# Forty lo subtractions and eight block additions go from VectorE to GpSimd

## Chip, cores and metric

The kernel runs on one core of a Trainium2 chip. The metric is the device time of one launch in microseconds (us). A core has five engines, each with its own in-order instruction queue: TensorE (PE, matmuls), VectorE (DVE), ScalarE (ACT), GpSimd (POOL) and SyncE (SP, which here only issues DMA transfers). ACT and POOL issue transfers too. An instruction that waits holds up everything behind it in its queue.

## The reference, cut to what matters

One layer of a streaming encoder with D = T = 1024 and float32 throughout:

```python
h = rms_norm(x, norm_mix_g) * (1.0 + sc1) + sh1
b_s, c_s, v_s, v_c, gl_c, gate_br = split(h @ w_in)
y_a = (b_s * causal_dwconv(c_s * v_s, conv_short_w)) @ w_short_out
u = causal_dwconv(v_c * sigmoid(gl_c), conv_conf_w) + conv_conf_b
y_b = silu(layer_norm(u, conf_ln_g, conf_ln_b)) @ w_conf_out
g_a, g_b = split(sigmoid(gate_br))
x = x + g1 * ((g_a * y_a + g_b * y_b) @ w_o)
...
x = x + g2 * ((silu(a) * bgate) @ w_ffn_out)
```

The change is in the two branch projections, `y_a` and `y_b`, and in the mix, the product with `w_o`.

## The kernel before

**Products in parts.** A float32 product is made of three matmuls in the fast format fp32r: operand and weight are each split into a hi part (the rounded value) and a lo part (what the rounding left), and hi x hi, hi x lo and lo x hi are added up in PSUM (`mm3`, L380, L381, L383). For a weight block, `split_w` makes the parts: ACT casts the loaded block (tile `raw`) to `wh` (L226), and `lo_engine` subtracts it from the block to make `wl` (L227). There are three buffers for `wh`, three for `wl` and five for `raw` in a ring; a new part waits until the product that used its buffer is through, and a new load waits until the last reader of its `raw` is.

**Products of seven.** The combined projection, the first branch projection, and the feed-forward block do a 2 x 2 block product with seven products of halves instead of eight (Strassen in Winograd's form). The names "1" to "7" in `PRODUCTS = "1265734"` are these. Some need sums of weight blocks, so a unit of the plan is a load, perhaps block additions, a hi cast and a lo subtraction. The first branch projection has two halves `d`, each with its seven: `ya_order` runs "1", "1", "2", "2" of both, then "6", "5", "7", "3", "4" of the first half and of the second. `apart_units` (L298) makes its units: two additions before "6", one each before "7" and "3" (all in `add`, L304).

**The plan.** `plan` is a list of weight units in the order of use. `next_w` hands out the next and keeps `AHEAD = 2` more made ahead. The kernel's program order is then rearranged by a scheduler that decides each engine's queue; semaphores keep the dependencies.

**The stages around the change** (times of the profile before). To 565.6 us: the combined projection, whose weights' lo parts are made by POOL, while DVE does the width-31 convolution (`conv`, L902, accumulators in PSUM). 565.6 to 645.6: the first branch projection, 14 products of 24 matmuls. In it DVE splits the operands (`q_split`, L850) and does their sums (`q_sum`), prepares the layer norm (`ln_square`: L945, L951; `ln_rstd`) and evacuates products (`ya_evac`: L737, L740, L744), with gate values `ga` that POOL's queue loads (L1016). The first half's products "2", "5" and "3" share one pair of banks (called y and z), products "6", "7", "4" another (x). 645.6 to 732.6: the second branch projection in two halves of 512 columns (`row_blocks`): eight weight units for the first half, of which three are kept, and five more for the second. Before each product `act_b` scales an operand (L982, with `rl0` for the first half and `rl1` for the second), applies silu on ACT and splits it (L413). `load_b` and `modulation_of` (L361) use DVE and the `raw` buffers for unrelated modulation sums. The gate loads `gb` (L1072, POOL's queue) take six shared small buffers (`gs`), two of which hold `rl0` and `rl1` until their last use. 732.6 to 820.5: the mix, 16 products, with loads of `xr` (L1087) and stores of the result (L1095) on POOL's queue. Then the feed-forward block, which the change leaves alone.

Of the kernel before, what the change touches and what calls it, by code (L numbers as in the profile page):

```python
# [44 lines left out]
KC = D // P  # L45
# [29 lines left out]
KEPT = 3  # L75
SECOND = [*range(KC - KEPT, KC), *range(KC - KEPT)]
# [51 lines left out]
def block_kernel(ctx: ExitStack, tc: tile.TileContext, x0, xT, c, vecs, ada, w_first, w_plain, w_duals,  # L128
                 w_short, w_conf, w_o, w_fi, w_fo, w_last, outT):
    nc = tc.nc  # L130
# [74 lines left out]
    def raw_tile(n=1024):  # L205

        raws.append(raws.pop(0))
        return raws[-1].tile([P, 1024], F32, tag="raw", name="raw")[:, :n]

    def load(src, n=1024):  # L210
        raw = raw_tile(n)
        load.ins = nc.sync.dma_start(raw, src).ins
        return raw
# [6 lines left out]
    def split_w(raw, n, after=(), lo_engine=nc.vector):  # L220
        wh = whp.tile([P, 1024], F32R, tag="wh", name="wh")[:, :n]
        wl = wlp.tile([P, 1024], F32R, tag="wl", name="wl")[:, :n]
        with ExitStack() as order:
            for ins in after:
                order.enter_context(tc.issue_after(ins))
            hi = nc.scalar.copy(wh, raw)  # L226
            lo = lo_engine.tensor_tensor(wl, raw, f32(wh), ALU.subtract)  # L227
        split_w.hi, split_w.lo = hi.ins, lo.ins
        if n == T and lo_engine is nc.gpsimd:
            pool_los.append((hi.ins, lo.ins))  # L230
        return wh, wl
# [66 lines left out]
    def apart_units(mats, eng):  # L298


        a = {}

        def add(out, x, y):
            eng.tensor_tensor(out, x, y, ALU.add)  # L304
            return out

        def get(b):
            return load(mats[("11", "12", "21", "22").index(b)])

        def unit(m):  # L310
            if m in "12":
                raw = get("1" + m)
            elif m == "6":
                for b in ("21", "22", "11"):
                    a[b] = get(b)
                a["s1"] = add(a["22"], a["21"], a["22"])
                raw = a["s2"] = add(raw_tile(), a["11"], a["s1"])
            elif m == "7":
                raw = add(a["21"], a["21"], a["11"])
            elif m == "3":  # L320
                raw = get("12")
                add(raw, raw, a["s2"])
            else:
                raw = a["s1"] if m == "5" else get("22")
            return split_w(raw, 1024, (), eng)

        return {m: (lambda m=m: unit(m)) for m in PRODUCTS}


    plan = [None] * KC  # L330
# [2 lines left out]
        units = dual_units([w_duals[d, m] for m in range(4)], 1024, eng=nc.gpsimd)  # L333
        plan += [units[m] for m in PRODUCTS]
    ya_order = [(d, m) for m in "12" for d in range(2)] + [(d, m) for d in range(2) for m in PRODUCTS[2:]]
    ya_units = [apart_units([w_short[d, m] for m in range(4)], nc.vector) for d in range(2)]
    plan += [ya_units[d][m] for d, m in ya_order]
    plan += [(w[k], 1024) for w in (w_conf, w_o) for ks in (range(KC), SECOND[KEPT:]) for k in ks]
    ready = []

    def next_w(ahead=AHEAD):
# [1195 lines left out]
```

## Time and profile before

| | before |
|---|---|
| device time, median of 3 | 1471.18 us (1470.85 to 1472.19) |
| span of the profiled execution, first to last instruction | 1469.8 us |
| mean granted TensorE clock | 0.998 |
| GpSimd busy | 515.7 us |
| VectorE busy | 1178.7 us |

The span is the time from the first instruction of the profiled execution to its last; its own device time is not listed apart, and the median of the runs lies 1.4 us above the span. Groups are read as: line, engine, operation, tiles written and read, shapes and count; then busy time and mean ns of one; then the idle time of the engine before them and what ended it. Rows of the timeline give the start, the length, the engine and the instructions (several of one kind in a row are merged). Rows of a window table give from and to, the length, then busy time and count of PE, weight loads (PEld), DVE, ACT and POOL, the granted clock, the DMA share and GB/s. A row of waits says who waited for what: us in total, times, longest.

### The profile page before, as it was taken

The page shows a single profiled execution, that of the slowest core. Times are in us where ns is not written, and L with a number is a line of the kernel's source. Part 1 is how long each engine was busy: PE and PEld are TensorE (multiplying, and loading weights), DVE is VectorE, ACT ScalarE, POOL GpSimd, SP SyncE. Part 2 cuts the span into 40 slices and gives each one's busy share as a digit, 9 for nine tenths or more (in the row PEclk, how much of TensorE's full clock was granted, in tenths as well). Part 3 has the DMA queues.
Part 4 walks back from the last instruction along what each step waited for, and adds up shares of the span by engine and source line. Part 5 has one row for each costly group of instructions (what it writes and reads, how often), then busy time and mean ns, then how long its engine had stood idle before and what let it go on. Part 6 is the DMA issues. An engine that isn't in the chain of part 4 may idle for free.

```text
span 1469.8 us, 17768 instructions
## 1 busy us (share of the span) xinstructions
PE 1459.0 (99%) x6447; PEld 1197.9 (81%) x6447; DVE 1178.7 (80%) x1625; ACT 615.0 (42%) x896; POOL 515.7 (35%) x464
## 2 busy tenths in 40 slices
PE   9999999999999999999999999999999999999997
PEld 5888888888888888888888888888888888888887
DVE  8999888887998969999688798777777765676755
ACT  5753433333433346455235474444444443222325
POOL 0046677767777771111022002101111115435005
PEclk9999999999999999999999999999999999999999
DMA  9412213222222258376596336654555449999403
GB/s 373 165 59 72 101 58 129 72 86 101 101 67 78 93 205 303 115 239 215 194 315 221 106 106 233 221 170 163 168 185 173 158 154 373 341 287 280 139 15 115
DMA packets 83913, 247.97 MB, mean 169 GB/s; under 512 B 9665, under 2 KB 11713, under 8 KB 83826
## 3 DMA queue, kind: packets, MB, share of 16 engines
q1 hardware_dynamic: 43072, 138.63, 28.3%
q0 software_dynamic: 37008, 95.63, 19.8%
q10 hardware_dynamic: 3746, 12.59, 2.3%
q8 instruction: 50, 0.82, 0.2%
q14 instruction: 37, 0.30, 0.1%
HBM read 184.41 MB, written 62.39 MB: 168 GB/s over the span
## 4 chain that ended last, share of the span: by engine, by line
PE 97%; DVE 1%; POOL 0%; issue 0%; ACT 0%; POOLq 0%; DVEq 0%
PE bank L383 12%; PE bank L380 12%; PE bank L381 12%; PE x L381 8%; PE x L383 8%; PE x L380 7%; PE z L380 4%; PE z L383 4%; PE z L381 4%; PE y L381 3%; PE y L380 3%; PE y L383 3%; PE mix L383 2%; PE mix L380 2%; PE yb L383 2%; PE yb L380 2%
## 5 line engine op out<-in xcount | busy, mean ns | idle before, releaser
L226 ACT CAST wh<-raw 128x1024 fp32r<-128x1024 f32 (+2 forms) x253 | 255.2, 1010 | 454.9 <-PE bank L381 129.9
L227 POOL TENSOR_TENSOR wl<-raw,wh 128x1024 fp32r<-128x1024 f32 x84 | 204.8, 2446 | 82.1 <-ACT wh L226 82.1
L227 DVE TENSOR_TENSOR wl<-raw,wh 128x1024 fp32r<-128x1024 f32 (+2 forms) x169 | 193.6, 1146 | 37.4 <-ACT wh L226 36.1
L902 DVE SCALAR_TENSOR_TENSOR c<-diff,vec,c 128x512 f32<-128x512 f32 x232 | 171.0, 752 | 4.4
L1250 POOL DMA_DIRECT2D hid<-stage x71 | 37.9, 534 | 345.4 <-DVE stage L421 341.1
L380 PE MATMUL bank<-th,wh 128*128 128x512 f32 x288 | 112.0, 389 | 0.0
L381 PE MATMUL bank<-tl,wh 128*128 128x512 f32 x288 | 112.0, 389 | 0.0
L383 PE MATMUL bank<-th,wl 128*128 128x512 f32 x288 | 112.0, 389 | 0.0
L902 DVE SCALAR_TENSOR_TENSOR c<-u,wsum,c 128x512 f32<-128x512 f32 x112 | 84.3, 753 | 2.6
L420 ACT CAST stage<-g 128x512 fp32r<-128x512 f32 x62 | 38.4, 622 | 84.0 <-DVE g L1239 41.9
L246 POOL TENSOR_TENSOR raw<-raw 128x1024 f32<-128x1024 f32 x12 | 29.2, 2433 | 125.1 <-DVE wl L227 87.7
L421 DVE TENSOR_TENSOR stage<-g,stage 128x512 fp32r<-128x512 f32 x62 | 42.4, 689 | 26.9 <-ACT stage L420 26.8
L381 PEld LDWEIGHTS bank<-tl,wh 128*128 128x128 f32 x288 | 54.1, 188 | 11.3
L383 PEld LDWEIGHTS bank<-th,wl 128*128 128x128 f32 x288 | 54.1, 188 | 11.2
L380 PEld LDWEIGHTS bank<-th,wh 128*128 128x128 f32 x288 | 54.1, 188 | 11.2
L1276 POOL DMA_DIRECT2D th<-hid x71 | 38.1, 537 | 52.8 <-PE x L383 29.3
L380 PE MATMUL x<-th,wh 128*128 128x512 f32 x144 | 56.1, 390 | 0.1
L383 PE MATMUL x<-th,wl 128*128 128x512 f32 x144 | 56.0, 389 | 0.0
L381 PE MATMUL x<-tl,wh 128*128 128x512 f32 x144 | 56.0, 389 | 0.0
L246 DVE TENSOR_TENSOR raw<-raw 128x1024 f32<-128x1024 f32 (+1 forms) x17 | 19.2, 1129 | 42.2 <-DMA raw<-in_w_fi 31.6
L380 PE MATMUL yb<-zsh,wh 128*128 128x512 f32 x128 | 49.8, 389 | 0.0
L381 PE MATMUL yb<-zsl,wh 128*128 128x512 f32 x128 | 49.8, 389 | 0.0
(811 smaller groups left out, 4243.9 us busy)
## 6 DMA issues: line engine op xcount, KB each, us to landing
hid<-stage POOLq DMA_DIRECT2D x71, 512.0 KB, 4.6
raw<-in_w_fi SPq DMA_DIRECT2D x54, 512.0 KB, 4.4
raw<-in_w_duals SPq DMA_DIRECT2D x48, 512.0 KB, 3.5
th<-hid POOLq DMA_DIRECT2D x71, 256.0 KB, 5.7
tl<-hid POOLq DMA_DIRECT2D x71, 256.0 KB, 5.7
ada<-in_ada SPq DMA_DIRECT2D x24, 512.0 KB, 5.5
raw<-in_ada SPq DMA_DIRECT2D x24, 512.0 KB, 4.5
raw<-in_w_fo SPq DMA_DIRECT2D x24, 384.0 KB, 5.8
```

Of the source, the lines that this page charges most:

```text
L226: hi = nc.scalar.copy(wh, raw)
L227: lo = lo_engine.tensor_tensor(wl, raw, f32(wh), ALU.subtract)
L246: eng.tensor_tensor(a["s1"], a["21"], a["22"], ALU.add)
L380: nc.tensor.matmul(ps, wh, xh, start=first, stop=False, skip_group_check=again)
L381: nc.tensor.matmul(ps, wh, xl, start=False, stop=False, skip_group_check=again)
L383: mm3.ins = nc.tensor.matmul(ps, wl, xh, start=False, stop=last, skip_group_check=again).ins
L420: t_split.act = nc.scalar.copy(hi, src).ins
L421: t_split.ins = nc.vector.tensor_tensor(lo, src, f32(hi), ALU.subtract).ins
L902: tap.ins = nc.vector.scalar_tensor_tensor(out=out, in0=src[:, s : s + H], scalar=wt, in1=acc, op0=ALU.mult, op1=ALU.add).ins
L1250: nc.gpsimd.dma_start(hid_dram[key], s)
L1276: nc.gpsimd.dma_start(t, hid_dram[key][:, s])
```

## The change

```diff
     ya_order = [(d, m) for m in "12" for d in range(2)] + [(d, m) for d in range(2) for m in PRODUCTS[2:]]
-    ya_units = [apart_units([w_short[d, m] for m in range(4)], nc.vector) for d in range(2)]
+    ya_units = [apart_units([w_short[d, m] for m in range(4)], nc.gpsimd) for d in range(2)]
     plan += [ya_units[d][m] for d, m in ya_order]
-    plan += [(w[k], 1024) for w in (w_conf, w_o) for ks in (range(KC), SECOND[KEPT:]) for k in ks]
+    plan += [(w[k], 1024, (), nc.gpsimd) for w in (w_conf, w_o) for ks in (range(KC), SECOND[KEPT:]) for k in ks]
```

The engine that `apart_units` hands to its additions and to `split_w` is GpSimd instead of VectorE, and the units of `w_conf` and `w_o` name GpSimd as the engine of their lo part. The hi casts stay on ACT, the loads on SP. That is 14 + 13 + 13 = 40 subtractions and 2 x 4 = 8 additions, each on 128 x 1024 elements. The scheduler places them in GpSimd's queue among the transfers that it issues; the order of VectorE's other work changes a little with it.

## The prediction

> **What bounds the kernel now.** I read the busy times and the chain of waits first, then who TensorE (PE) waits for.
>
> ```profile
> PE 1459.0 (99%) x6447; PEld 1197.9 (81%) x6447; DVE 1178.7 (80%) x1625; ACT 615.0 (42%) x896; POOL 515.7 (35%) x464
> PE 97%; DVE 1%; POOL 0%; issue 0%; ACT 0%; POOLq 0%; DVEq 0%
> ```
> ```profile
> PE clock L573 <- DVE ones_r L591: 1.6, 1, 1.6
> PE x L381 <- DVE t4l L421: 0.5, 1, 0.5
> PE clock L573 <- DVE newton L450: 0.2, 1, 0.2
> ```
>
> PE is on the chain for 97% of the span, and the three rows are all that it waits for: 2.3 us, none of it in the stages that the change touches. The busy times of these stages, as windows (PE, weight loads, VectorE = DVE, ScalarE = ACT, GpSimd = POOL): two windows of the first branch projection, two halves of the second, two of the mix.
>
> ```profile
> 565.50:594.50 29.00, 29.00 (x126) 23.31 (x125) 28.82 (x41) 21.49 (x38) 2.18 (x4) 1.00 0.72 248
> 594.50:645.50 51.00, 51.00 (x221) 41.12 (x220) 48.70 (x68) 26.19 (x36) 7.53 (x14) 1.00 0.52 170
> 645.50:689.00 43.50, 43.50 (x193) 36.02 (x193) 42.83 (x66) 24.93 (x35) 3.65 (x7) 1.00 0.74 240
> 689.00:732.50 43.50, 43.50 (x194) 36.02 (x193) 31.52 (x47) 13.78 (x19) 3.88 (x8) 1.00 0.59 194
> 732.50:776.00 43.50, 43.50 (x194) 36.02 (x193) 35.12 (x58) 13.69 (x19) 8.67 (x16) 1.00 0.84 288
> 776.00:820.50 44.50, 44.50 (x196) 36.49 (x195) 32.82 (x43) 24.12 (x34) 8.13 (x15) 1.00 0.65 209
> ```
>
> PE is full and at full clock everywhere, so there is nothing to win. DVE is full too until 689, with little slack towards PE, while POOL is nearly free. The question is whether POOL can take the work without making DVE late.
>
> **What it costs DVE when POOL computes.** POOL did such subtractions before, in the combined projection. In the first fence are POOL's and DVE's operations of all times, in the second those between 543.5 and 557.4, where POOL's last ones of that stage meet DVE work with two inputs in SBUF; the third has the same DVE forms some microseconds later, with POOL idle.
>
> ```profile
> L227 POOL TENSOR_TENSOR wl<-raw,wh 128x1024 fp32r<-128x1024 f32 x84 | 204.8, 2446 | 82.1 <-ACT wh L226 82.1
> L902 DVE SCALAR_TENSOR_TENSOR c<-diff,vec,c 128x512 f32<-128x512 f32 x232 | 171.0, 752 | 4.4
> ```
> ```profile
> L850 DVE TENSOR_TENSOR q<-q,q1h 128x512 fp32r<-128x512 f32 x4 | 6.9, 1786 | 0.0
> L425 DVE SCALAR_TENSOR_TENSOR q<-q,q 128x512 f32<-128x512 f32 x4 | 6.9, 1775 | 0.0
> L227 POOL TENSOR_TENSOR wl<-raw,wh 128x1024 fp32r<-128x1024 f32 x3 | 8.2, 2753 | 7.3 <-ACT wh L226 7.3
> L923 POOL TENSOR_TENSOR tot<-tot,u 128x512 f32<-128x512 f32 x2 | 3.4, 1742 | 0.0
> ```
> ```profile
> 558.61 2.48 DVE L425 SCALAR_TENSOR_TENSOR q<-q,q 128x512 f32<-128x512 f32 x4
> 587.14 2.49 DVE L850 TENSOR_TENSOR q<-q,q3h 128x512 fp32r<-128x512 f32 x4
> ```
>
> Four such operations take 2.5 us alone (0.6 each) and 6.9 us beside POOL. The eight lost 13.8 - 4.8 = 9.0 us to three long and two short POOL operations; shared out by these lengths (2753 to 1742) that is 2.1 us for each long one. POOL loses only 2753 - 2446 = 0.3 us. The two engines alternate: one DVE operation gets through for each POOL operation. The convolution's taps (L902, accumulator in PSUM, 752 ns through all that POOL did) are not touched, so operations with an operand in PSUM are free of it. In the stages of the change most DVE work is of the endangered kind: the q splits (L850), L945, L951, L982, L413, L1061.
>
> [...]
>
> **What moves.** 40 subtractions (14 for the first projection, 13 each for the second and the mix) and 8 block additions. Rows of DVE between 557.4 and 591.8:
>
> ```profile
> L227 DVE TENSOR_TENSOR wl<-raw,wh 128x1024 fp32r<-128x1024 f32 x6 | 7.3, 1215 | 0.0
> L304 DVE TENSOR_TENSOR raw<-raw 128x1024 f32<-128x1024 f32 x4 | 4.9, 1218 | 0.2 <-DMA raw<-in_w_short 0.2
> ```
>
> DVE is freed of 1.14 us each (1.22 less the 0.08 in which neighbours overlap): 55 us. POOL gets 48 x 2.45 = 118 us, and each costs DVE 2.1 us wherever DVE has no gap: a net loss of 1.0 us each. Removed ACT work, PE work, loads: none. In the changed order the additions and subtractions also share POOL's queue with the gate loads (L1016, L1072), the x loads (L1087) and the x1 stores (L1095), which wait for buffers and results.
>
> **First place: the second use of the y banks.** Product "5" of the first half (starts at 594.53) writes the bank that L740 must have read.
>
> ```profile
> 557.41 1.28 DVE L737 TENSOR_TENSOR sig<-bank,sig 128x512 f32<-128x512 f32 x2
> 571.10 1.21 DVE L304 TENSOR_TENSOR raw<-raw 128x1024 f32<-128x1024 f32 x1
> 591.88 1.28 DVE L740 TENSOR_TENSOR ma<-bank,ga 128x512 f32<-128x512 f32 x2
> 607.32 1.28 DVE L737 TENSOR_TENSOR z<-bank,vz 128x512 f32<-128x512 f32 x2
> ```
> ```profile
> 594.53 0.39 PE L380 MATMUL bank<-q5h,wh 128*128 128x512 f32 x1
> 610.91 0.39 PE L380 MATMUL bank<-q4h,wh 128*128 128x512 f32 x1
> ```
> ```profile
> 578.42 28.16 SPq L212 DMA_DIRECT2D raw<-in_w_short  x6
> ```
>
> Slack today: 594.5 - 592.5 (end of L740's first) = 2 us. In the new order 40 DVE operations stand between 557.4 and L740: 24.1 us. Six subtractions and four additions of POOL come with them: two before 571, when the first addition can run (today's L304), then eight in a row, 8 x 2.8 = 22 us, until 593.5. Three more follow before DVE is through: the seventh subtraction, the next half's first addition, the eighth subtraction; the SP row says that raw buffers are short, so they come with gaps. L740 then runs at 557.4 + 24.1 + 13 x 2.1 = 608.8, and PE waits 608.8 - 594.5 = **14.3 us**. Low end: ten POOL operations, four DVE ones with PSUM hidden under them: 557.4 + 24.1 + 21 - 2.4 = 600.1, a wait of 5.6. High end: fourteen, 16.4.
>
> **Second place: product "4" of the first half**, due 16.4 us after product "5", writes the x bank that L737 (607.32 now) must have read. 25 DVE operations stand between: 15.1 us, with four or five POOL operations, 9.5 us, less 1.2 hidden: 23.4 - 16.4 = **7.0 us** more. Low 1 (one POOL operation), high 10. After it POOL waits for gate loads whose buffers DVE frees, and DVE catches up: I cost the way to the second projection at nothing. Its cover is the slack of zsl, 645.55 - 640.34 = 5.2 us; without it each POOL operation there costs 2.1 us less 1.1.
>
> ```profile
> 639.65 0.69 DVE L413 TENSOR_TENSOR zsl<-cv,zsh 128x512 fp32r<-128x512 f32 x1 [0.18 <-ACT zsh L412]
> ```
> ```profile
> 645.55 0.39 PE L380 MATMUL yb<-zsh,wh 128*128 128x512 f32 x1
> 679.33 0.39 PE L383 MATMUL yb<-zsh,wl 128*128 128x512 f32 x1
> ```
>
> **Third place: the last subtraction of the second projection's first half** now stands in POOL's queue behind the sixth gate load, which waits until DVE has used rl1 for the last time (L982).
>
> ```profile
> 645.97 1.31 DVE L744 SCALAR_TENSOR_TENSOR ma<-bank,ga 128x512 f32<-128x512 f32 x2 [0.91 <-DMA ga<-gate_a]
> 676.90 3.10 DVE L982 TENSOR_TENSOR cv<-cv,rl1r 128x512 f32<-128x512 f32 x5
> 680.30 0.54 POOL L1072 DMA_DIRECT2D gb<-gate_b  x1 [16.73 <-DVE cv L982]
> ```
> ```profile
> L227 DVE TENSOR_TENSOR wl<-raw,wh 128x1024 fp32r<-128x1024 f32 x6 | 7.3, 1221 | 0.0
> ```
>
> PE needs it at 679.33 of today's clock; that load goes out at 680.30 today. The six subtractions in this stretch (last row, 645.9 to 680.1) leave DVE: 680.0 - 6.8 = 673.2. Five POOL operations come in: + 10.5 = 683.7, then the load's issue and the subtraction, 0.5 + 2.4: 686.6, a wait of **7.3 us**. Low 0 (no POOL operation in DVE's way), high 11 (six and a blocked L361, whose inputs are both in SBUF; it never met POOL before).
>
> **Mix.** 13 operations at a net 1.0 us are 13 us, and DVE has 8.4 + 11.7 = 20 us of gaps in these two windows; each subtraction stands behind the x1 store of two or three products earlier, a slack of at least one product (a third of 16.4 us). I take 0, at most 4.
>
> **Sum.** 14.3 + 7.0 + 7.3 = 28.6 us on the span of 1469.8, which lies 1.4 below the median of 1471.2: **1500 us**. The ends: 1471.2 + 6.6 = 1478 and 1471.2 + 41.4 = 1513.
>
> **Rivals.**
> - Not slower: in the first projection DVE keeps its place and POOL is the one that waits (0.3 us each), so that DVE is 25 us earlier there and PE stays full. That gives 1470.5 to 1471.2: PE's waits leave at most 0.5 us to win. It decides at L740: no later than 592 us. For it: DVE issues a new operation every 0.6 us. Against: L850 at 1786 ns in the same setting. [...]
> - Small: the collision is there, but DVE, freed of 11.4 us before L740, waits anyway for ACT and PE, and POOL's turns fall into these gaps. Then only the low ends count: about 6.6 us, 1478. For it: DVE's new idle time; against: most of the 24 us ahead of L740 are splits whose operands lie ready.
> - Worse: the waits feed back. Gate loads held up by late DVE hold POOL's queue, subtractions come late for PE, raw buffers come free late, and SP's weight loads with them. The highs and one more product's 5.4 us in four places: 41 + 22 = 63 us, 1534. For it: 28.16 us for six loads on SP's queue today; against: 22 operations of 2.8 us are 62 of the first projection's 80 us, so POOL itself keeps up.
>
> **Chances.** Forecast 0.74, not slower 0.09, small 0.09, worse 0.08. A measurement here tells 0.2% (2.9 us) from no change. Slower by more: 0.91; within: 0.07; faster: 0.02. The range 1478 to 1520 holds the forecast's ends, most of the small case and part of the worse, about 0.8.
>
> **What will show it.** L850 and L945 near 1.8 to 2.8 us between 560 and 610, L740 near 609, PE waits on DVE before q5 and q4 products of the first half, and on POOL's wl in the second projection. The forecast is wrong if L850 stays near 0.68 us, if PE's product pitch stays at (610.91 - 594.53) / 3 = 5.46 us throughout, or if the loss sits in the mix.

## The result: slower, and the profile after

| | before | after |
|---|---|---|
| device time, median | 1471.62 us (1470.85 to 1472.19, 4 runs) | 1512.63 us (1511.41 to 1517.9, 4 runs) |
| span of the profiled execution | 1469.8 us | 1511.6 us |
| mean granted TensorE clock | 0.998 | 0.988 |

The ratio is 1.028, with a 95% interval of 1.027 to 1.030. The forecast was 1500, its range 1478 to 1520.

The page of the changed kernel: busy times, and the chain of waits by engine.

```profile
PE 1471.6 (97%) x6447; PEld 1204.5 (80%) x6447; DVE 1181.8 (78%) x1577; ACT 615.2 (41%) x896; POOL 648.0 (43%) x512
PE 48%; DVE 5%; POOL 4%; issue 3%; DMA 2%; ACT 1%; POOLq 0%; SPq 0%; DVEq 0%; ACTq 0%
```

DVE gave up 48 operations and yet is busier than before (1181.8 to 1178.7 us): its other operations became longer. PE's busy time has also grown, by 12.6 us, for the same 6447 matmuls. Whom PE waits for (us in total, times, longest):

```profile
PE bank L383 <- POOL wl L227: 17.0, 4, 7.1
PE yb L380 <- ACT wh L226: 4.9, 1, 4.9
PE mix L383 <- POOL wl L227: 2.8, 1, 2.8
PE bank L380 <- DVE ma L740: 1.9, 1, 1.9
...
PE yb L383 <- POOL wl L227: 1.2, 1, 1.2
PE yb L381 <- DVE zsl L413: 0.6, 1, 0.6
```

These new waits add up to 28.4 us (three smaller new ones, 1.1 us together, are not shown); the span grew by 41.8. Most of the rest shows in the granted clock. Windows (from and to, length, busy time and count of PE, PEld, DVE, ACT, POOL, then the clock): the six stretches at half clock inside the run, each of which begins during one of these waits or within 1.3 us after it, and one window at full clock.

```profile
581.73:588.56 6.83, 4.09 (x10) 3.22 (x11) 0.09 (x1) 1.66 (x3) 6.75 (x4) 0.50 0.10 16
605.63:609.04 3.41, 3.41 (x9) 2.67 (x8) 3.41 (x7) 2.94 (x5) 2.48 (x1) 0.50 0.34 126
622.69:629.52 6.83, 4.63 (x11) 3.67 (x12) 0.00 (x0) 0.00 (x0) 6.81 (x5) 0.50 0.15 52
643.17:646.58 3.41, 3.41 (x10) 2.67 (x9) 0.00 (x0) 0.29 (x1) 3.39 (x3) 0.50 0.91 304
711.44:718.27 6.83, 4.40 (x10) 3.01 (x11) 1.38 (x2) 1.79 (x3) 2.47 (x2) 0.50 0.67 236
807.01:810.42 3.41, 3.41 (x9) 2.63 (x9) 0.79 (x5) 0.00 (x0) 2.44 (x2) 0.50 0.59 213
592.00:598.83 6.83, 6.83 (x32) 5.66 (x31) 6.83 (x3) 4.07 (x8) 6.82 (x5) 1.00 0.26 89
```

Counted as these windows count, with the matmuls that an edge cuts, a matmul takes 6.83 / 32 = 0.213 us of PE at full clock. In the six stretches 59 of them took 23.35 us, 0.396 each: 59 x 0.183 = 10.8 us lost to the clock. (From start to start the matmuls of this trace lie 0.227 us apart at full clock and 0.427 at half; that gives 10.9.) Waits and clock make 39.2 of the 41.8 us. The busy times add up in full: PE's busy time grew by 12.6 us and its idle time by 29.2 (from 1469.8 - 1459.0 to 1511.6 - 1471.6).

Where PE lost it, from the starts of the same matmuls in both traces: the end of the first branch projection came 27.0 us later than before, that of the second 37.4, that of the mix 42.6; from there on nothing is lost.

Two of the long waits come about in the same way. GpSimd's queue in the first projection (start, length, operation, and in brackets the idle time before it with what ended it):

```profile
574.58 7.54 POOL L304 TENSOR_TENSOR raw<-raw 128x1024 f32<-128x1024 f32 x1 [3.64 <-DMA raw<-in_w_short]
582.09 2.33 POOL L227 TENSOR_TENSOR wl<-raw,wh 128x1024 fp32r<-128x1024 f32 x1
584.50 2.37 POOL L304 TENSOR_TENSOR raw<-raw 128x1024 f32<-128x1024 f32 x1
...
590.46 2.77 POOL L304 TENSOR_TENSOR raw<-raw 128x1024 f32<-128x1024 f32 x1 [1.25 <-DMA raw<-in_w_short]
...
606.56 5.40 POOL L227 TENSOR_TENSOR wl<-raw,wh 128x1024 fp32r<-128x1024 f32 x1 [1.45 <-ACT wh L226]
...
615.49 7.05 POOL L304 TENSOR_TENSOR raw<-raw 128x1024 f32<-128x1024 f32 x1 [3.53 <-DMA raw<-in_w_short]
622.50 2.34 POOL L227 TENSOR_TENSOR wl<-raw,wh 128x1024 fp32r<-128x1024 f32 x1
```

What DVE did during the first of the two long additions:

```profile
573.83 1.28 DVE L850 TENSOR_TENSOR q6l<-q,q6h 128x512 fp32r<-128x512 f32 x2
575.03 2.49 DVE L850 TENSOR_TENSOR q5l<-q,q5h 128x512 fp32r<-128x512 f32 x4
577.44 2.49 DVE L850 TENSOR_TENSOR q7l<-q,q7h 128x512 fp32r<-128x512 f32 x4
```

And what PE did:

```profile
584.47 0.80 PE L383 MATMUL bank<-q2h,wl 128*128 128x512 f32 x1 [6.04 <-POOL wl L227]
```

The addition waits 3.64 us for its load and starts during the second of ten splits of DVE, which have two inputs in SBUF. DVE runs them at 0.6 us each, as if alone, until 579.93; the addition, 2.4 us long when nothing disturbs it, ends 2.2 us after DVE's last one. Behind it in the queue stands the subtraction for product "2", which needed no addition at all. PE waits 6.04 us for it. At 615.49 the same happens with the addition for product "3": it ends 2.2 us after DVE's last operation with two inputs in SBUF (L945, until 620.34), though DVE then goes on with L737, which reads PSUM. PE waits 7.1 us for the subtraction of 622.50. The subtraction of 606.56 (5.40 us) also ends 2.3 us after such a run. The addition of 590.46 does not wait for the end: it gets in after the DVE operation that was running, and DVE's next one takes 2.9 us.

The late addition also reaches DVE, through ScalarE's queue. A hi cast there waits for the next addition, which stands behind the subtraction of 582.09 and runs from 584.50 to 586.87:

```profile
586.90 1.05 ACT L226 CAST wh<-raw 128x1024 fp32r<-128x1024 f32 x1 [11.46 <-POOL raw L304]
```

In the kernel before, this cast ran at 578.48, after a wait of 4.05 us for DVE's addition. Behind it in ScalarE's queue stand the means (`mu`, L936) that DVE's next operation reads, so DVE is idle for 8.55 us, until 588.48.

So the collision is there, and GpSimd loses by it too. The groups of both engines in the first projection (count, then busy us and mean ns of one), and three of DVE's in the kernel before:

```profile
L304 POOL TENSOR_TENSOR raw<-raw 128x1024 f32<-128x1024 f32 x8 | 29.3, 3661 | 15.3 <-DMA raw<-in_w_short 11.5 <-PE bank L383 3.7
L227 POOL TENSOR_TENSOR wl<-raw,wh 128x1024 fp32r<-128x1024 f32 x10 | 28.2, 2816 | 1.5 <-ACT wh L226 1.4
```
```profile
L951 DVE TENSOR_TENSOR sq<-sq 128x512 f32<-128x512 f32 x14 | 14.4, 1041 | 1.4 <-ACT sq L947 1.4
L945 DVE TENSOR_TENSOR cv<-cv,mu 128x512 f32<-128x512 f32 x16 | 13.0, 855 | 8.5 <-ACT mu L936 8.5
L850 DVE TENSOR_TENSOR q<-q,q3h 128x512 fp32r<-128x512 f32 x4 | 7.6, 1950 | 0.0
```
```profile
L945 DVE TENSOR_TENSOR cv<-cv,mu 128x512 f32<-128x512 f32 x16 | 10.3, 681 | 0.0
L951 DVE TENSOR_TENSOR sq<-sq 128x512 f32<-128x512 f32 x14 | 9.2, 681 | 0.0
L850 DVE TENSOR_TENSOR q<-q,q3h 128x512 fp32r<-128x512 f32 x4 | 2.5, 681 | 0.0
```

GpSimd's additions lost 3661 - 2450 = 1.2 us each, its subtractions 0.37 (2450 ns is the mean that the prediction took from the kernel before); DVE's undisturbed value is the 681 of the kernel before.

### The profile page after: what moved, and what is told of

Read it like the earlier page. It is cut to its first block, busy times and chain, and to the rows that moved or that the text cites. A ratio compares the mean times of both kernels' runs of the same rounds, so it can differ in the third digit from the quotient of the medians.

```text
span 1511.6 us, 17800 instructions
## 1 busy us (share of the span) xinstructions
PE 1471.6 (97%) x6447; PEld 1204.5 (80%) x6447; DVE 1181.8 (78%) x1577; ACT 615.2 (41%) x896; POOL 648.0 (43%) x512
## 3 DMA queue, kind: packets, MB, share of 16 engines
q0 software_dynamic: 37008, 95.63, 18.9%
## 4 chain that ended last, share of the span: by engine, by line
PE 48%; DVE 5%; POOL 4%; issue 3%; DMA 2%; ACT 1%; POOLq 0%; SPq 0%; DVEq 0%; ACTq 0%
PE x L381 7%; PE x L383 7%; PE x L380 7%; PE z L383 3%; PE z L380 3%; PE z L381 3%; PE y L383 3%; PE y L380 3%; PE y L381 3%; POOL wl L227 2%; POOL raw L304 1%; PE yb L383 1%; DVE raw L361 1%; PE yb L380 1%; PE yb L381 1%
## 5 line engine op out<-in xcount | busy, mean ns | idle before, releaser
L227 POOL TENSOR_TENSOR wl<-raw,wh 128x1024 fp32r<-128x1024 f32 x124 | 308.9, 2498 | 127.9 <-ACT wh L226 127.5
L227 DVE TENSOR_TENSOR wl<-raw,wh 128x1024 fp32r<-128x1024 f32 (+2 forms) x129 | 146.2, 1133 | 30.2 <-ACT wh L226 29.2
L246 POOL TENSOR_TENSOR raw<-raw 128x1024 f32<-128x1024 f32 x12 | 29.2, 2430 | 124.2 <-DVE wl L227 87.3
L421 DVE TENSOR_TENSOR stage<-g,stage 128x512 fp32r<-128x512 f32 x62 | 42.4, 689 | 28.3 <-ACT stage L420 28.2
L383 PE MATMUL yb<-zsh,wl 128*128 128x512 f32 x128 | 50.7, 396 | 1.2 <-POOL wl L227 1.2
```

The source lines that it names most:

```text
L246: eng.tensor_tensor(a["s1"], a["21"], a["22"], ALU.add)
L383: mm3.ins = nc.tensor.matmul(ps, wl, xh, start=False, stop=last, skip_group_check=again).ins
L421: t_split.ins = nc.vector.tensor_tensor(lo, src, f32(hi), ALU.subtract).ins
```

## The experiments

Each kernel differs from the kernel before or from the changed one by the edit shown, which is cut to the lines that matter. "First", "second" and "mix" are the us by which PE fell behind the kernel before within that stage, by the starts of the first matmul of the next one (for the mix: of the kernel's last matmul, with what was lost behind it). Stages that an edit leaves alone differ by up to 1 us. Each stage's figure comes from one execution, and the runs of one kernel with waits in the first projection differ by up to 6.5 us (the changed kernel's by 1511.4 to 1517.9), so 2 or 3 us more or less in a stage are not firm.

| run | median, us | ratio to before (95%) | first | second | mix |
|---|---|---|---|---|---|
| changed kernel | 1512.63 | 1.0284 (1.0272 to 1.0296) | 27.0 | 10.4 | 4.4 |
| first projection alone | 1496.44 | 1.0168 (1.0145 to 1.0190) | 23.7 | 0 | -0.8 |
| second projection alone | 1482.56 | 1.0074 (1.0058 to 1.0089) | 0.7 | 11.9 | 0.7 |
| mix alone | 1478.49 | 1.0040 (1.0027 to 1.0052) | 1.0 | 0 | 5.8 |
| first, subtractions alone | 1483.01 | 1.0074 (1.0059 to 1.0089) | 10.6 | 0 | 0.1 |
| first, additions alone | 1481.67 | 1.0065 (1.0048 to 1.0082) | 10.2 | 0 | 0 |
| changed, other splits | 1511.36 | 1.0267 (1.0252 to 1.0282) | 21.1 | 11.4 | 7.7 |
| both engines subtract | 1521.27 | 1.0336 (1.0315 to 1.0358) | 24.7 | 15.2 | 11.6 |
| halves shared | 1487.83 | 1.0109 (1.0093 to 1.0124) | 9.0 | 5.9 | 2.3 |
| second, cast first | 1476.23 | 1.0030 (1.0018 to 1.0042) | 0.2 | 3.7 | 0.7 |
| second, gate load free | 1482.88 | 1.0075 (1.0060 to 1.0090) | 0.7 | 10.6 | -0.7 |
| second, both of these | 1475.78 | 1.0022 (1.0012 to 1.0032) | 1.0 | 2.5 | 0.2 |
| mix, stores on ScalarE | 1480.91 | 1.0058 (1.0041 to 1.0075) | -0.3 | 0 | 10.1 |

### One stage at a time

First projection alone: `ya_units` with `nc.gpsimd`, the plan's line as before.

> Only the units of the first branch projection (14 subtractions, 8 additions) are on GpSimd; the second projection and the mix stay on VectorE. In the changed kernel the end of the first projection came 27.0 us later than before, and from there to the end of the mix another 15.6 us went. If each place pays for its own units (my theory: the lo parts come late from GpSimd's queue, and each wait of TensorE is followed by a stretch at half clock), this kernel is 27 us slower than before (1496 to 1500) with the whole delay there at the end of the first projection. If the later places lose only because the first one has upset the queues and the buffers (rival: feedback), it is 35 to 43 us slower.

Second projection alone, and with the two engines exchanged the mix alone:

```diff
-    plan += [(w[k], 1024) for w in (w_conf, w_o) for ks in (range(KC), SECOND[KEPT:]) for k in ks]
+    plan += [(w[k], 1024, (), e) for w, e in ((w_conf, nc.gpsimd), (w_o, nc.vector)) for ks in (range(KC), SECOND[KEPT:]) for k in ks]
```

> Only the 13 subtractions of the second projection are on GpSimd. My theory: 8 to 11 us slower than before (1479 to 1483), nearly all at the last unit of its first half, whose subtraction waits behind the sixth gate load on GpSimd's queue and whose hi cast waits on ScalarE; the row of waits names ACT wh or POOL wl there. Rival (feedback from the first projection): within 2 us of before.

> Only the 13 subtractions of the mix are on GpSimd. My theory: 3 to 5 us slower than before (one subtraction behind a store in GpSimd's queue, one TensorE wait of about 3 us and one stretch of 3.4 us at half clock). Rival (feedback, or a place that only the shifted times of the changed kernel hit): within 1 us of before.

The three lose 24.7, 10.9 and 6.8 us against the before of their own runs, together 42.4 for the change's 41.0. Within the scatter of the runs the stages do not upset one another; each pays for its own units, and feedback from one stage to the next is not needed. (Feedback inside a stage is not excluded by this.) The mix alone is dearer than expected by 2 us: beside the 2.3 us for POOL's wl, PE waited 2.0 us for a sum of squares (L1102) that DVE made late.

### Subtractions or additions

In the first projection only the subtractions, or only the additions, are GpSimd's. The first is made from the changed kernel by this edit, with the plan's line as before; the second from the kernel before, with `nc.gpsimd` in the same place:

```diff
         def add(out, x, y):
-            eng.tensor_tensor(out, x, y, ALU.add)
+            nc.vector.tensor_tensor(out, x, y, ALU.add)
```

> Of the first projection only the 14 subtractions are on GpSimd; the 8 block additions stay on VectorE. If GpSimd is late because load, addition, addition, cast and subtraction follow one another on an engine that takes 2.4 us for each (my theory), the waits at the products that need sums shrink, and the kernel is 5 to 15 us slower than before instead of 27. [...]

> Of the first projection only the 8 block additions are on GpSimd, the subtractions stay on VectorE, second projection and mix as before. If the delay of the first projection (24 us with all 22 operations there, 10.6 us with the subtractions alone) comes from chains of addition and subtraction that follow one another in one slow queue, the additions alone cost less than the missing 13 us: 3 to 10 us. If each operation costs on its own, wherever the next one runs, they cost 12 to 15 us.

14 subtractions lose 10.6 us in the stage, 8 additions 10.2, all 22 operations 23.7. The parts make 20.8 of the 23.7 us, 0.8 us per subtraction and 1.3 per addition wherever the next one runs; the 10.2 lie between the two expectations, and the 2.9 us that are left for chains that only the whole has are within the scatter. But no wait was the same in both: with the subtractions alone the wait before product "2" is gone, and PE waits 2.1 us for L740 and 2.0 for ScalarE; with the additions alone it waits 4.4 us for ScalarE and 2.6 for a wl of DVE. In that kernel one addition took 13.48 us, after a wait of 9.51 us for DVE:

```profile
565.41 13.48 POOL L304 TENSOR_TENSOR raw<-raw 128x1024 f32<-128x1024 f32 x1 [9.51 <-DVE sig L737]
```

The wait of 4.4 us for ScalarE follows from it: a hi cast waited 9.72 us for GpSimd's additions, and the copy that PE needed (L1025) stood behind the cast. The order in GpSimd's, DVE's and ScalarE's queues decides where the loss falls.

### Taking the run of splits away

The changed kernel with shorter DVE operations in place of the operand splits, so that DVE's run is over earlier:

```diff
-                nc.vector.tensor_tensor(lo, f32(src), f32(hi), ALU.subtract)
+                nc.vector.tensor_scalar(lo, f32(hi), 0.0, None, ALU.mult)
```

> The changed kernel, but VectorE makes the lo parts of the first projection's operands (line 850) as the hi part times zero, with one input from SBUF in place of two; so the lo parts of these operands are left out of the result. [...] Theory of the queue alone (GpSimd waits for the load and everything stands behind it): the wait before product 2 stays at 5 us or more, and the end stays at 24 to 28 us.

GpSimd's queue:

```profile
575.75 2.40 POOL L304 TENSOR_TENSOR raw<-raw 128x1024 f32<-128x1024 f32 x1 [3.79 <-DMA raw<-in_w_short]
578.11 2.34 POOL L227 TENSOR_TENSOR wl<-raw,wh 128x1024 fp32r<-128x1024 f32 x1
```

The addition of the same place, which again waited for its load (3.79 us), took 2.40 us instead of 7.54. PE's matmul with the wl of product "2" started 2.43 us after the one before it instead of 6.43. So 4 of these 6 us were the addition held off by DVE; the rest is the late load and GpSimd's length of operation. The author had estimated a wait of at most 1.5 us and a delay of 10 to 20 us if DVE's run is what holds the addition off; of the first projection's 27.0 us only 5.9 went, and 21.1 are left. (The time hardly moved, because second projection and mix lost 4 us more in this run.) One input did not make the other splits immune: three of them took 6.45 us together beside GpSimd at 589.8.

### The collision without a late lo part

The kernel before, where GpSimd subtracts once more what DVE has already subtracted:

```diff
+        split_w.hi, split_w.lo = hi.ins, lo.ins; lo_engine or nc.gpsimd.tensor_tensor(raw, raw, f32(wh), ALU.subtract)
```

> VectorE makes all 40 lo parts and all additions as before, and GpSimd does each of the 40 subtractions again, into the loaded block, where nobody waits for the result but the buffer's next load (and the second addition to it before product 3, whose weights are changed by that and so is the result). If what costs is the lateness of the lo part on GpSimd, this kernel loses 0 to 4 us. [...]

It loses 49.4 us, more than the change. Whom PE waits for, the two largest rows:

```profile
PE yb L383 <- DVE wl L227: 7.0, 1, 7.0
PE bank L383 <- DVE wl L227: 5.5, 4, 3.3
```

and two groups of DVE in the first projection:

```profile
L227 DVE TENSOR_TENSOR wl<-raw,wh 128x1024 fp32r<-128x1024 f32 x15 | 21.9, 1463 | 0.0
L945 DVE TENSOR_TENSOR cv<-cv,mu 128x512 f32<-128x512 f32 x16 | 15.9, 1033 | 0.0
```

Not one of its waits is for GpSimd, whose results nobody needs but the next load into the block. GpSimd computing beside a DVE that has no slack, and holding the blocks longer (the run doesn't separate the two), is enough to lose as much; here DVE is the late one (1463 ns where it took 1217, 1033 where it took 681). In the change DVE has 1.14 us less to do for each operation, and the loss shows up at GpSimd instead.

### Half of each operation on each engine

```diff
-            lo = lo_engine.tensor_tensor(wl, raw, f32(wh), ALU.subtract)
+            lo = [e.tensor_tensor(wl[:, s], raw[:, s], f32(wh)[:, s], ALU.subtract) for e, s in ((nc.vector, halves[0]), (nc.gpsimd, halves[1]))][1] if lo_engine is None else lo_engine.tensor_tensor(wl, raw, f32(wh), ALU.subtract)
```

(and the same for the additions).

> Each of the 40 subtractions and 8 additions is shared: VectorE makes columns 0 to 511, GpSimd columns 512 to 1023. GpSimd's part of one operation should take about 1.36 us (its 128x512 addition of line 923 before) instead of 2.4, VectorE gets some 0.6 us for each. If the change costs because one operation takes GpSimd twice as long and the next of its chain waits for it, the kernel loses less than half of the 41 us: 1475 to 1490. [...]

```profile
L227 POOL TENSOR_TENSOR wl<-raw,wh 128x512 fp32r<-128x512 f32 x15 | 32.2, 2155 | 22.3 <-ACT wh L226 22.2
L304 POOL TENSOR_TENSOR raw<-raw 128x512 f32<-128x512 f32 x8 | 12.5, 1570 | 14.4 <-DMA raw<-in_w_short 10.9 <-DVE wl L227 1.9 <-DVE q L850 1.4
```
```profile
PE bank L380 <- DVE z L737: 4.6, 2, 3.9
```

The loss falls from 41 to 15.6 us, within the range of the theory of the late lo part, though not by the durations it gave: a half subtraction took GpSimd 2.16 us, not 1.36; why is not shown. Addition and subtraction together went from 3.66 + 2.82 = 6.5 us to 3.7. No wait for GpSimd is left; the largest one that remains (last row) is for DVE, which now does half the work and still meets GpSimd as often. A fixed price for each meeting of the two engines does not fit. A price that goes by the length of GpSimd's operation, as the prediction shared it out, would fall by half as well, and this run does not tell it from the theory of the late lo part.

### The last unit of the second projection's first half

PE's matmuls of products 6 and 7, which run as one, wait here for the last unit's wh and wl (4.9 and 1.2 us). Two things stood in front of it: its hi cast in ScalarE's queue behind silus of the second half (L983), which wait for DVE's L982; and its subtraction in GpSimd's queue behind the sixth gate load, which waits for the last L982 too. ScalarE's queue in the kernel before, where this cast stands ahead of those silus, and in the changed kernel:

```profile
672.73 1.05 ACT L226 CAST wh<-raw 128x1024 fp32r<-128x1024 f32 x1 [2.43 <-PE yb L381]
677.63 3.65 ACT L983 ACTIVATE cv<-cv,vec 128x512 f32<-128x512 f32 x5 [3.85 <-DVE cv L982]
```
```profile
710.16 1.52 ACT L983 ACTIVATE cv<-cv,vec 128x512 f32<-128x512 f32 x2 [5.07 <-DVE cv L982]
711.58 1.03 ACT L226 CAST wh<-raw 128x1024 fp32r<-128x1024 f32 x1
```

One kernel moves the cast ahead, one frees the gate load, one does both:

```diff
-        nc.scalar.activation(z, z, AF.Silu, bias=col(V_LNB, k), scale=col(V_LNG, k))
+        with tc.issue_after(kept_hi[-1]) if h and len(kept_hi) == KEPT else ExitStack(): nc.scalar.activation(z, z, AF.Silu, bias=col(V_LNB, k), scale=col(V_LNG, k))
```
```diff
-            rs.append(rstd_start(var, eps2, f"rl{h}"))
+            rs.append(rstd_start(var, eps2, f"rl{h}", tile_of=s_tile))
```

> Second projection alone on GpSimd, as in the run with 1482.56 us, but the silus of the second half's operands are put behind the hi cast of the first half's last unit in ScalarE's queue. If that cast, standing in ScalarE's queue behind silus that wait for VectorE, is what is late (my reading now), TensorE's 4.9 us wait for wh goes and the kernel is at 1472 to 1476. If the sixth gate load in front of the subtraction in GpSimd's queue is what is late (the prediction's step), the wait is the same 5 to 7 us with POOL wl in place of ACT wh, and the time stays at 1480 to 1484.

> Second projection alone on GpSimd (1482.56 us), but the two factors rl0 and rl1 lie in other buffers, so that the sixth gate load no longer waits for their last use by line 982; the orders of VectorE's, ScalarE's and SyncE's queues are the same. If the prediction's step was right (the last subtraction waits behind that load), the wait at the last unit of the first half goes from 6 us to at most 1 and the time to 1472 to 1476. If the hi cast in ScalarE's queue is what is late, nothing changes: 1480 to 1484, wait for ACT wh 4.9 us.

> Both together: the silus behind the cast, and the factors in other buffers. With the cast in time (1476.23 us) GpSimd's queue still stood 3.85 us for the gate load before the last two subtractions. If that was the rest of the wait, TensorE's 1.3 us for POOL wl there goes too: 1473 to 1475, with only the wait of about 2 us at the first operands left. If it was not, 1476 stays.

With the gate load freed and nothing else changed, GpSimd no longer stands for it, but for the cast; the time does not move, and PE waits as long as with the second projection alone (4.9 us for wh, 1.2 for wl):

```profile
686.33 2.35 POOL L227 TENSOR_TENSOR wl<-raw,wh 128x1024 fp32r<-128x1024 f32 x1 [5.47 <-ACT wh L226]
```
```profile
PE yb L380 <- ACT wh L226: 4.9, 1, 4.9
```

With the cast ahead and the gate load as it was, ScalarE casts at 674.76 (at 685.68 without the edit), and only 1.3 us for wl are left; GpSimd's row shows it standing for the load:

```profile
677.41 0.56 POOL L1072 DMA_DIRECT2D gb<-gate_b  x1 [3.85 <-DVE cv L982]
677.99 4.75 POOL L227 TENSOR_TENSOR wl<-raw,wh 128x1024 fp32r<-128x1024 f32 x2
```

With both, GpSimd does three subtractions in a row from 671.39, no wait is left at this unit, and the stage loses 2.5 us instead of 11.9. By the time alone, 1475.78 us is not told from the 1476.23 with the cast ahead, and it lies above the 1473 to 1475 expected; that the wait is gone is read from the trace. (The first edit also moved two L982 on DVE ahead of the modulation sums, so it isn't the cast's place alone.) So the gate load is real but second: 1.3 us behind a cast that cost 4.9.

### The stores of the mix

```diff
-        nc.gpsimd.dma_start(x1_dram[j][:, halves[h]], dst)
         sq = nc.scalar.activation(xr, dst, AF.Square, scale=1.0 / 32.0)
+        nc.scalar.dma_start(x1_dram[j][:, halves[h]], dst)
```

> Mix alone on GpSimd (1478.49 us), but its stores (line 1095) go through ScalarE's queue, right behind the square that waits for the same result. If the subtraction is late because it stands behind a store in GpSimd's queue, TensorE's 2.3 us wait for POOL wl in the mix goes, and the time is 1472 to 1475. If not, it stays at 1476 to 1479.

GpSimd's queue in the mix alone:

```profile
766.13 0.54 POOL L1095 DMA_DIRECT2D x_dram<-x  x1 [2.81 <-DVE x L1092]
766.69 2.36 POOL L227 TENSOR_TENSOR wl<-raw,wh 128x1024 fp32r<-128x1024 f32 x1
```

and with the stores on ScalarE:

```profile
763.62 0.56 POOL L1087 DMA_DIRECT2D xr<-in_xT  x1 [4.89 <-DVE xr L1102]
764.20 2.38 POOL L227 TENSOR_TENSOR wl<-raw,wh 128x1024 fp32r<-128x1024 f32 x1
```

The expectation failed: the next transfer in the queue, a load of `xr` whose buffer DVE frees, takes the store's place, and PE waits 3.1 us in two places for POOL's wl instead of 2.3 in one. So the store is not the cause by itself: the load behind it in the same queue, which also waits for DVE, delays the subtraction as well. The time, 1480.91 us, lies above both ranges: PE also waits 3.1 us for the sum of squares (L1102; 2.0 with the stores on GpSimd), and 3.0 of the 10.1 us were lost behind the mix, for reasons that were not followed up.

## Why the prediction held, point by point

**The verdict and its premise** were right: PE was full, nothing could be won, and each stage that got GpSimd work lost time. The sum was 28.6 us; the new waits of PE are 28.4. That agreement is luck in the largest stage, for the places within a stage were not those named. By stage the waits were 18.9 us in the first projection (forecast 14.3 + 7.0), 6.7 in the second (7.3) and 2.8 in the mix (0). Of the signs that the prediction named, L850 near 1.8 to 2.8 us shows in one group of six ("q3h", 1950 ns); one more took 1147, and four stayed at 0.68 us, which it had named as a sign of being wrong.

**"POOL loses only 0.3 us"** is the step that failed. It came from subtractions beside DVE operations that alternated with them, and DVE's price of 2.1 us was taken from there for the whole kernel. In the first projection DVE's three groups above lost 14 x 0.36 + 16 x 0.17 + 4 x 1.27 = 12.8 us beside 18 GpSimd operations, and three smaller groups some 6 more: about 1 us for each. It had been freed of 1.14 us for each, and its own work did not make it late: it even stood idle for 8.55 us. GpSimd lost 8 x 1.2 + 10 x 0.37 = 13 us, and PE waited for it. Who loses differs from place to place. At 574.58, 606.56 and 615.49 an operation of GpSimd that came while DVE ran back to back waited for the end of the run; at 590.46 another got in after one DVE operation. What decides between the two is not shown. The alternation is there as well, where DVE's operations come while GpSimd is at work without a break: L850 for "3" at 1950 ns.

**First place, L740.** L740 ran at 603.60 (forecast 608.8), and PE waited 1.9 us for it, not 14.3. The start of product "5" came 604.42 - 594.53 = 9.9 us late all the same, inside the 5.6 to 16.4 given; 6.04 of it was the wait for the wl of product "2", which the prediction did not have, with the half clock behind it; that the size fits is luck. Nor was L740 late in the way forecast, by DVE's lengthened operations alone: it ran 11.7 us later than before, and ahead of it DVE stood idle for 8.55 us, because ScalarE's cast waited for GpSimd's addition.

**Second place, L737, and the way on "at nothing".** L737 of the changed kernel was not waited for (with the first projection alone it was, for 3.9 us). From product "5" to the end of the stage 27.0 - 9.9 = 17.1 us went instead of 7.0, mostly in three waits for GpSimd's wl: of "3" of the first half, behind the addition that took 7.05 us, of "4", and of "6" of the second half. The reason not followed up was in the prediction's own case "worse": GpSimd's additions waited 11.5 us for loads.

**Third place.** The size was right (waits of 4.9 + 1.2 us for a forecast 7.3) by luck, the cause was not: the gate load stands in the queue as described, but freeing it changed nothing, for the hi cast was later still, in ScalarE's queue, for the same L982; once the cast was in time, the gate load was worth 1.3 us. The prediction looked at the queues that gained instructions and left out one whose order had shifted.

**Mix.** A slack of one product was too little where a store waits for DVE's evacuation: 2.8 us of waiting, outside the 0 but inside the 4; the stage lost 4.4 us with the clock.

**What was missing from the sum** is the clock: 10.8 of the 13.2 us by which the result (41.8 us by spans) lies above 28.6. A wait of PE was priced at its own length. In the trace the waits of 1.9, 3.0 and 2.8 us were each followed by 3.41 us at half clock, and during those of 6.0, 7.1 and 4.9 us a stretch of 6.83 us began.

**The rivals.** "Not slower" had the right observation, that GpSimd is the one that waits, and the wrong consequence: what GpSimd loses PE gets, because the lo parts are due within two units. "Small" (1478) is refuted by the time: DVE's idle time was there, but it came from the lateness of GpSimd's addition. "Worse" (feedback, 1534) is refuted as a sum, and between stages by the three separate runs; within the first projection parts of it are there, such as a gate load that left late from GpSimd's queue and for which DVE then stood 9.2 us (L744, until 630.13).

**What stays open.** How the 27.0 us of the first projection divide between late loads, the length of GpSimd's operations and DVE's runs beside them is known only for one wait. More buffers for the loaded blocks, which would test the loads, were not tried. What the clock costs was worked out, not measured by itself. No version beat the kernel before, and none could by much with PE at 99%.

## What to carry to other kernels

An operation that takes another engine twice as long (here 2.45 us on GpSimd for 1.22 on DVE) isn't free because that engine is idle: ask when its result is due, what stands before it in that engine's queue, and which transfers in that queue wait for whom. If two engines slow each other down, as these two did (a split of DVE 1950 ns for 681, an addition of GpSimd 7.54 us for 2.45), price the collision for both, and look for runs of back-to-back operations, during which the other engine may get nothing (here the addition ended 2.2 us after DVE's run). Follow a late result into the queues of the engines that wait for it: here a cast that waited in ScalarE's queue held up what DVE needed next. Where the bound engine was never idle before, count each new wait with the half clock that may follow it: here six waits of 1.9 to 7.1 us came with six stretches of 3.41 or 6.83 us, which cost 10.8 us beside the 28.4 of the waits.

## Hardware behaviour not expected

- A GpSimd addition of 2.4 us took 7.54 and 7.05 us beside an unbroken run of DVE operations with two SBUF inputs, which themselves ran at their full pace (one every 0.6 us, 128 x 512 each). Both ended 2.2 us after the last such operation. With the additions alone one took 13.48 us. It does not always go so: at 590.46 GpSimd got in after one operation of a run, took 2.77 us, and DVE's next operation took 2.88. The prediction had seen only the opposite, DVE losing 2.1 us for each GpSimd operation.
- The clock was halved for 3.41 or 6.83 us at a time, and not with the longest waits alone: in the changed kernel a matmul that started 2.25 us after the one before it was followed by a stretch of 3.41 us, and so was one that started 3.17 us after. In the mix with stores on ScalarE, gaps of 1.50, 2.41 and 3.48 us had none (mean granted clock 0.999). So in these runs a PE that stood for some 2 to 3.5 us paid in some places and not in others; what decides is not shown.
